# Delta-rule sum tables of a two-block model made by ScalarE copies instead of VectorE products

## The chip, the core and the metric

The kernel runs on one core of a Trainium2 chip. The metric is the device time of one execution in microseconds; the time of a kernel is the median of its runs.

## The reference, cut to what matters

Two transformer blocks follow one another over 512 tokens of width 1024, all in float32. The first block mixes tokens in two ways at once: a gated delta rule (4 heads of 128, chunks of 64 tokens) and a sparse attention (compressed, selected and windowed keys), followed by a feed-forward part. The second block is attention with relative bias, a convolution, and a feed-forward part. The change touches the delta rule, of which this is the part that matters:

```python
gcum = jnp.cumsum(chunks(g), axis=-1)
gdiff = gcum[..., :, None] - gcum[..., None, :]
dec_strict = jnp.where(strict, jnp.exp(jnp.where(strict, gdiff, 0.0)), 0.0)
dec_incl = jnp.where(incl, jnp.exp(jnp.where(incl, gdiff, 0.0)), 0.0)
lower = bc[..., None] * jnp.einsum('nbhid,nbhjd->nbhij', kc, kc) * dec_strict
gam = jnp.exp(gcum)
...
qk = jnp.einsum('nbhid,nbhjd->nbhij', qc, kc) * dec_incl
q_dec = qc * gam[..., None]
```

Here g is one number per token and head (the log of a decay), and gcum its running sum in a chunk. The exponentials of its differences weigh the products of keys and queries.

## The kernel before, in words

Nearly every large product is made on TensorE (PE) from operands split in two: a rounded high part (`whi`, made by ScalarE from the loaded chunk `raw`, L238) and the rest (`wlo`, made by VectorE, L241), so that one product is three matmuls. Weights come in 512 KB chunks from HBM into three buffers of `raw` (`load`, `chunk`, L282).

The delta rule's preparation is a loop over `c`, four chunks of 128 tokens (L886 on). For each it transposes the keys (`kT`, L888), takes the squares of their norms (`rsq`, L878: four small ScalarE squares, a power on GpSimd), and makes the table `rg`: for each of the two parts of g (high and rest, `g2`, L697) and each of the 4 heads, the upper triangle of ones times that head's column of g, 128x128. Four matmuls read the table (`sums_of_g`, L899): two with ones as the other operand give the running sums (`gb`, whose exponential is `gB`, L910), two with a lower triangle give the differences (`gd`, whose exponential is `dm`, L915). PSUM tag `pv` has two buffers, and `rg` has one. Further on in the same step, ScalarE copies the transposed weighted keys (`kbF`, L921; shown in the trace as `h<-tp`), PE makes `qk` and `kk`, and VectorE weighs them with `dm`; the last of these (`a<-sc,dm`, L939 and L940) gives the triangular system that is solved next.

Into this loop, a generator (`side`, L853) mixes independent work in portions: the input products of the sparse attention. Its first part, `nsa_blocks` (L771), makes two products, copies each by ScalarE into four shifted pieces (L782 to L785, `a<-mm` in the trace), adds positions by VectorE (L795, `a<-a,n`), and multiplies the result with the compress weights straight from `raw` (L805, `mm<-raw,a`, 64 matmuls).

The program text gives the priorities, but the order of the instructions on each engine is planned at build time by the framework, which simulates the program (`schedule_with_timeline_sim=True`). On the chip each engine then works through its list in order. Helpers record their own line: nearly all ScalarE work has L238 (`act`), all products and sums of two tensors L241 (`tt`), so tiles tell the steps apart.

Of the kernel before, what the change touches and what calls it, by code (L numbers as in the profile page):

```python
# [6 lines left out]
F32 = mybir.dt.float32  # L7
F32R = mybir.dt.float32r
AF = mybir.ActivationFunctionType
ALU = mybir.AluOpType  # L10
# [191 lines left out]
def body(tc, nc, A, dbg=None, upto=99):  # L202
# [13 lines left out]
    def sb(pool, shape, dt=F32, tag=None, bufs=1):  # L216
        if tag is None:
            nx[0] += 1
            return pool.tile(list(shape), dt, name=f"n{nx[0]}", bufs=bufs)
        return pool.tile(list(shape), dt, name=tag, tag=tag, bufs=bufs)  # L220
# [7 lines left out]
    def ps(tag, shape=(128, 512)):  # L228
        return pp.tile(list(shape), F32, name=tag, tag=tag, bufs=2)
# [7 lines left out]
    def act(out, in_, f, **k):  # L237
        return ACT.activation(out, in_, f, **k)  # L238

    def tt(out, a, b, op, e=None):  # L240
        return (e or DVE).tensor_tensor(out, a, b, op=op)  # L241

    def ts(out, a, s0, s1, op0, op1=None):
        return DVE.tensor_scalar(out, a, s0, s1, op0=op0, op1=op1) if op1 else DVE.tensor_scalar(out, a, s0, None, op0=op0)

    def stt(out, a, s, b, op0, op1):
        return DVE.scalar_tensor_tensor(out, a, s, b, op0=op0, op1=op1)  # L247

    def mm(out, l, r, start=True, stop=True, **k):
        return PE.matmul(out, lhsT=l, rhs=r, start=start, stop=stop, **k)  # L250

    def bc(ap, shape):
        return ap.to_broadcast(shape)
# [354 lines left out]
    B4 = [128, 4, 128]  # L608
# [20 lines left out]
    def r4(ap):  # L629
        return ap.rearrange("p (h c) -> p h c", h=4)  # L630

    def b4(ap):
        return bc(ap[:, :, None], B4)
# [30 lines left out]
    G = {k: ap.bitcast(F32) for k, ap in GR.items()}  # L664
# [31 lines left out]
    g2 = sb(pA, [128, 2, QT, 4], F32R)  # L696
# [163 lines left out]
    def tr4(src, e_out, tag):  # L860
        b = ps(tag, B4)
        for h in range(4):
            PE.transpose(b[:, h], src[:, h], ident)  # L863
        if e_out is not None:
            act(e_out, b, AF.Copy)
        return b

    def tok(c):
        return slice(c * 128, (c + 1) * 128)
# [4 lines left out]
    def pr(ap):  # L874

        return ap.rearrange("p a (h n) -> p a h n", h=2)

    def rsq(i, x):  # L878

        r2 = rqk[:, i, c]  # L880
        for h in range(4):
            act(sb(p1, [128, 128], F32, "jk", 2), x[:, h], AF.Square, accum_out=r2[:, h:h + 1])
        ts(r2, r2, 4 * EPS, None, ALU.add)
        POOL.tensor_tensor(r2, r2, mhalf[:, :4], op=ALU.pow)

    for c in range(QT):  # L886
        kF, qF, vF = (U[nm][:, :, tok(c)] for nm in "kqv")
        kT = tr4(kF, None, "sc")  # L888
        side.run(0.75)
        rsq(0, kT)  # L890
        knc = r4(kn[:, c])
        tt(knc, kT, b4(rqk[:, 0, c]), ALU.mult)
        kb = sb(p1, B4, F32, "h2", 2)
        tt(kb, knc, b4(beta[:, c]), ALU.mult, POOL)
        rg = sb(p1, [128, 2, 4, 128], F32R, "rg", 1)
        for i in range(2):
            tt(rg[:, i], bc(G["triu"][:, None, :], B4), b4(g2[:, i, c].bitcast(F32)), ALU.mult)

        def sums_of_g(o, l):  # L899
            for i in range(2):  # L900
                mm(o.rearrange("p h n -> p (h n)"), l, rg[:, i].rearrange("p h n -> p (h n)"),
                   start=i == 0, stop=i == 1)

        vT = tr4(vF, None, "sc")
        side.run(0.75)
        tt(r4(vb[:, c]), vT, b4(hb[:, c]), ALU.mult)
        gb = ps("pv", B4)
        sums_of_g(gb, GR["ones"])
        gB = sb(p1, B4, F32, "gB", 1)
        act(gB, gb, AF.Exp)  # L910
        side.run(0.75)
        gd = ps("pv", B4)
        sums_of_g(gd, GR["sl"])
        dm = sb(p1, B4, F32, "dm", 2)
        act(dm, gd, AF.Exp)  # L915
        side.run(0.75)
        tt(r4(qdF[:, c]), qF, gB, ALU.mult)
        for h in range(4):
            stt(dm[:, h], dm[:, h], rqk[:, 0, c, h:h + 1], G["triu"], ALU.mult, ALU.mult)
        kbF = sb(p1, B4, F32, "h2", 2)  # L920
        tr4(kb, kbF, "tp")  # L921
        side.run(0.75)
        qk = ps("pv", B4)
        for h in range(4):
            mm(qk[:, h], kF[:, h], qF[:, h])
        side.run(0.75)
        tt(r4(qkT[:, c]), qk, dm, ALU.mult)
        rsq(1, tr4(qF, None, "tp"))
        ts(rqk[:, 1, c], rqk[:, 1, c], 128.0 ** -0.5, None, ALU.mult)
        tt(rq2[:, c], rqk[:, 1, c], rqk[:, 1, c], ALU.mult)  # L930
        kk = ps("sc", B4)
        for h in range(4):
            mm(kk[:, h], kF[:, h], kbF[:, h])
        side.run(0.75)

        k2, d2 = (ap.rearrange("p (a h) n -> p a h n", a=2) for ap in (kk, dm))
        for i in range(2):
            hl = slice(64 * i, 64 * i + 64)
            tt(pr(qF[hl, 0:2]), k2[hl, :, :, hl], d2[hl, :, :, hl], ALU.mult)  # L939
        tt(pr(qF[0:64, 2:4]), k2[0:64, :, :, 64:], d2[0:64, :, :, 64:], ALU.mult)  # L940
# [496 lines left out]
    for t in range(4):  # L1437
# [11 lines left out]
        for qt in reversed(range(QT)):  # L1449
            W = (qt + 1) * 128  # L1450
            for g in range(2):
                h = 2 * t + g
# [126 lines left out]
```

## Time and profile before

| | us |
|---|---|
| median of 3 runs | 1549.27 |
| lowest and highest | 1548.56 and 1551.22 |
| the profiled execution | 1548.64 |
| its span | 1546.7 |
| TensorE busy in it | 1496.1 |
| VectorE busy | 938.5 |
| ScalarE busy | 673.2 |

The span is the time from the first to the last instruction that the profiler recorded. Busy times count instructions with work; a wait at the head of an instruction is idle time. In a timeline, neighbours of one kind are merged into one line, whose length is that of the whole group. The number in brackets is how long the engine stood before it, and after the arrow stands what ended that. The granted clock is 1.00 at TensorE's upper level (2.4 GHz) and 0.50 at the lower (1.2 GHz).

### The profile page before, as it was taken

How to read it: one execution, taken by the hardware profiler on the slowest of the kernel's cores; microseconds unless marked ns; L12 is line 12 of the kernel's file. 1: busy time of each engine (PE TensorE's matmuls, PEld its weight loads, DVE VectorE, ACT ScalarE, POOL GpSimd, SP SyncE). 2: the span in 40 equal slices, each digit the busy share in tenths (PEclk: the TensorE clock that was granted, in tenths of full speed). 3: DMA queues.
4: the chain of work that ended last, by engine and by line, in shares of the span. 5: the costliest groups of instructions: out<-in, count | busy, mean ns of one | idle time of the engine just before them, and what ended most of it. 6: DMA issues, size and time to landing. Idle time of an engine off the chain costs nothing.

```text
span 1546.7 us, 19932 instructions
## 1 busy us (share of the span) xinstructions
PE 1496.1 (97%) x7446; PEld 1255.2 (81%) x7446; DVE 938.5 (61%) x1599; ACT 673.2 (44%) x1250; POOL 145.1 (9%) x249
## 2 busy tenths in 40 slices
PE   7998999999999999999999999999989999999997
PEld 6876888888877878888888878888878888888876
DVE  5778754556647559865664456698844444444556
ACT  6443553345524334444454344345742433333434
POOL 2012001000000122200001010020100000000001
PEclk9999999999999999999999999999999999999999
DMA  6314211211044079933379643164610344434785
GB/s 213 97 53 150 69 56 55 69 42 42 1 164 150 30 259 342 323 111 95 109 270 354 260 150 96 55 231 137 244 42 14 116 140 140 143 121 141 270 283 207
DMA packets 65727, 225.85 MB, mean 146 GB/s; under 512 B 8088, under 2 KB 8088, under 8 KB 64864
## 3 DMA queue, kind: packets, MB, share of 16 engines
q1 hardware_dynamic: 47808, 159.27, 30.9%
q0 software_dynamic: 17248, 64.27, 11.5%
q8 instruction: 58, 0.95, 0.2%
q10 hardware_dynamic: 576, 1.05, 0.2%
q14 instruction: 37, 0.30, 0.1%
HBM read 190.73 MB, written 36.46 MB: 147 GB/s over the span
## 4 chain that ended last, share of the span: by engine, by line
PE 85%; DMA 5%; DVE 4%; ACT 3%; issue 1%; POOL 0%; SPq 0%; POOLq 0%; ACTq 0%; DVEq 0%
PE mm L250 34%; PE sc L250 17%; PE pv L250 16%; PE tp L250 15%; DMA raw<-W 2%; DMA raw<-T 2%; PE tp L1120 1%; DVE wlo L241 1%; ACT whi L238 1%; ACT a L238 1%; DVE a L241 1%; PE tp L619 1%; DMA x<-x 0%; PE tp L863 0%; DMA t<-W 0%
## 5 line engine op out<-in xcount | busy, mean ns | idle before, releaser
L238 ACT ACTIVATE whi<-raw 128x1024 fp32r<-128x1024 f32 (+1 forms) x223 | 232.2, 1043 | 411.4 <-issue 112.8
L241 DVE TENSOR_TENSOR wlo<-raw,whi 128x1024 fp32r<-128x1024 f32 (+2 forms) x209 | 250.5, 1201 | 238.1 <-ACT whi L238 229.6
L250 PE MATMUL mm<-a,whi 128*128 128x512 f32 x608 | 192.8, 396 | 1.1 <-ACT a L238 1.1
L250 PE MATMUL mm<-u,whi 128*128 128x512 f32 x544 | 175.5, 399 | 0.0
L250 PE MATMUL pv<-a,whi 128*128 128x512 f32 (+2 forms) x576 | 160.3, 362 | 1.8 <-ACT a L238 1.2
L250 PEld LDWEIGHTS mm<-a,whi 128*128 128x128 f32 x608 | 115.3, 191 | 25.3 <-ACT a L238 1.3
L250 PE MATMUL mm<-a,wlo 128*128 128x512 f32 x304 | 120.2, 395 | 3.0 <-DVE wlo L241 3.0
L250 PEld LDWEIGHTS pv<-a,whi 128*128 128x128 f32 x576 | 104.2, 189 | 18.9 <-ACT a L238 2.1
L250 PEld LDWEIGHTS mm<-u,whi 128*128 128x128 f32 x544 | 101.2, 190 | 19.4
L250 PE MATMUL tp<-a,whi 128*128 128x512 f32 x368 | 113.9, 390 | 0.0
L250 PE MATMUL mm<-u,wlo 128*128 128x512 f32 x272 | 107.6, 396 | 0.0
L250 PE MATMUL sc<-a,whi 128*128 128x512 f32 x336 | 104.3, 390 | 0.0
L250 PE MATMUL pv<-a,wlo 128*128 128x512 f32 (+2 forms) x288 | 103.7, 361 | 0.0
L247 DVE SCALAR_TENSOR_TENSOR n<-n,n,n 128x511 f32<-128x511 f32 (+23 forms) x120 | 84.6, 734 | 4.2 <-ACT n L238 2.3
L250 PEld LDWEIGHTS tp<-a,whi 128*128 128x128 f32 x368 | 69.1, 188 | 14.3
L250 PE MATMUL sc<-a 128*128 128x128 f32 (+4 forms) x288 | 71.5, 345 | 2.7 <-DVE st L1115 2.7
L250 PEld LDWEIGHTS sc<-a,whi 128*128 128x128 f32 x336 | 63.3, 188 | 13.1
L250 PE MATMUL tp<-a,wlo 128*128 128x512 f32 x184 | 71.6, 389 | 0.0
L250 PEld LDWEIGHTS mm<-a,wlo 128*128 128x128 f32 x304 | 57.9, 190 | 15.4 <-DVE wlo L241 3.4
L250 PEld LDWEIGHTS pv<-a,PT 128*128 128x128 f32 x480 | 63.5, 193 | 8.1 <-ACT PT L238 3.5
L250 PE MATMUL pv<-a,PT 128*128 128x64 f32 x480 | 64.2, 270 | 2.9 <-ACT PT L238 1.7
L250 PE MATMUL sc<-a,wlo 128*128 128x512 f32 x168 | 65.4, 389 | 0.0
(375 smaller groups left out, 2839.3 us busy)
## 6 DMA issues: line engine op xcount, KB each, us to landing
raw<-W SPq DMA_DIRECT2D x227, 512.0 KB, 3.7
a<-W SPq DMA_DIRECT2D x22, 512.0 KB, 6.2
low<-a POOLq DMA_DIRECT2D x22, 512.0 KB, 6.5
raw<-T SPq DMA_DIRECT2D x20, 512.0 KB, 4.8
S<-sp POOLq DMA_DIRECT2D x33, 256.0 KB, 3.2
wlo<-low POOLq DMA_DIRECT2D x14, 512.0 KB, 3.9
a<-S POOLq DMA_DIRECT2D x6, 1024.0 KB, 7.5
w<-W SPq DMA_DIRECT2D x22, 256.0 KB, 5.3
```

What stands on the lines that cost most here:

```text
L238: return ACT.activation(out, in_, f, **k)
L241: return (e or DVE).tensor_tensor(out, a, b, op=op)
L247: return DVE.scalar_tensor_tensor(out, a, s, b, op0=op0, op1=op1)
L250: return PE.matmul(out, lhsT=l, rhs=r, start=start, stop=stop, **k)
L619: PE.transpose(b[:, j, :], src[:, k * 128:(k + 1) * 128], ident)
L1120: PE.transpose(b[:, k * 128:(k + 1) * 128], p_[:, k * 128:(k + 1) * 128], ident)
```

## The change

The table is no longer made by two VectorE products for each chunk (one for each part of g, 128x512, the triangle and the column of g both broadcast), but by eight ScalarE copies, one for each part and head (128x128), each of which reads the triangle and multiplies it by the head's column of g as its scale. Shape, type and the single buffer of `rg` stay, and so does all that reads it.

```diff
@@ -894,7 +894,8 @@
         tt(kb, knc, b4(beta[:, c]), ALU.mult, POOL)
         rg = sb(p1, [128, 2, 4, 128], F32R, "rg", 1)
         for i in range(2):
-            tt(rg[:, i], bc(G["triu"][:, None, :], B4), b4(g2[:, i, c].bitcast(F32)), ALU.mult)
+            for h in range(4):
+                act(rg[:, i, h], G["triu"], AF.Copy, scale=g2[:, i, c, h:h + 1].bitcast(F32))
```

## Rows read from the trace of the kernel before

**Rows 1.** Busy line of the page: busy us, share of the span, instructions of each engine

```profile
PE 1496.1 (97%) x7446; PEld 1255.2 (81%) x7446; DVE 938.5 (61%) x1599; ACT 673.2 (44%) x1250; POOL 145.1 (9%) x249
```

**Rows 2.** Tile view of `rg`: count, ns min/median/max, first and last start, form

```profile
L241 DVE TENSOR_TENSOR rg<-n,n x8: 672/680/694, 100.3 to 126.5; 128x512 fp32r<-128x512 f32 x8
```

**Rows 3.** Windows: us, busy (count) of PE, PEld, DVE, ACT, POOL; clock; DMA, GB/s

```profile
100.00:105.00 5.00, 5.00 (x24) 4.06 (x24) 2.31 (x5) 0.55 (x5) 2.25 (x3) 1.00 0.01 3
105.00:110.00 5.00, 5.00 (x33) 4.30 (x31) 3.35 (x8) 2.17 (x8) 0.88 (x1) 1.00 0.00 0
110.00:115.00 5.00, 4.11 (x30) 3.34 (x29) 4.40 (x13) 4.88 (x13) 1.62 (x3) 1.00 0.00 0
115.00:120.00 5.00, 4.71 (x23) 2.89 (x22) 4.93 (x13) 2.40 (x11) 0.00 (x0) 1.00 0.32 93
...
125.00:130.00 5.00, 3.40 (x27) 2.83 (x26) 4.84 (x14) 3.06 (x16) 1.77 (x3) 1.00 0.32 101
...
140.00:145.00 5.00, 2.33 (x20) 1.93 (x19) 4.77 (x11) 4.37 (x18) 0.62 (x2) 1.00 0.82 232
145.00:150.00 5.00, 5.00 (x19) 3.78 (x18) 4.88 (x16) 0.40 (x4) 3.67 (x3) 0.66 0.63 202
```

**Rows 4.** PE timeline: start us, us, what [idle before <-releaser]

```profile
109.97 0.71 PE L250 MATMUL pv<-rg,n 128*128 128x512 f32 x2
...
111.76 0.71 PE L250 MATMUL pv<-rg,n 128*128 128x512 f32 x2
113.06 0.63 PE L863 MATMUL sc<-n,a 128*128 128x128 f32 x4 [0.58 <-DVE a L241]
...
115.45 1.72 PE L250 MATMUL mm<-raw,a 128*62 128x256 f32 x7 [0.29 <-DVE a L241]
...
126.03 1.16 PE L250 MATMUL pv<-a 128*128 128x128 f32 x8 [0.78 <-DVE a L241]
...
144.75 0.81 PE L863 MATMUL sc<-n,a 128*128 128x128 f32 x4 [2.67 <-DVE a L241]
```

**Rows 5.** DVE timeline, the same columns

```profile
112.84 1.06 DVE L241 TENSOR_TENSOR a<-a,n 128x248 f32<-128x248 f32 x2
...
114.23 0.68 DVE L241 TENSOR_TENSOR rg<-n,n 128x512 fp32r<-128x512 f32 x1
114.83 1.04 DVE L241 TENSOR_TENSOR a<-a,n 128x248 f32<-128x248 f32 x2
115.80 0.67 DVE L241 TENSOR_TENSOR rg<-n,n 128x512 fp32r<-128x512 f32 x1
...
125.90 1.28 DVE L241 TENSOR_TENSOR rg<-n,n 128x512 fp32r<-128x512 f32 x2
...
142.16 1.23 DVE L241 TENSOR_TENSOR wlo<-raw,whi 128x1024 fp32r<-128x1024 f32 x1
143.30 1.30 DVE L241 TENSOR_TENSOR a<-sc,dm 64x256 f32<-64x256 f32 x3
```

**Rows 6.** ACT timeline, the same columns

```profile
107.10 0.60 ACT L238 ACTIVATE gB<-pv 128x512 f32<-128x512 f32 x1 [6.55 <-PE pv L250]
107.60 0.59 ACT L238 ACTIVATE dm<-pv 128x512 f32<-128x512 f32 x1
108.92 0.60 ACT L238 ACTIVATE h<-tp 128x512 f32<-128x512 f32 x1 [0.73 <-PE tp L863]
...
110.44 1.81 ACT L238 ACTIVATE a<-mm 64x512 f32<-64x512 f32 x3
...
113.37 0.58 ACT L238 ACTIVATE gB<-pv 128x512 f32<-128x512 f32 x1
...
121.53 0.60 ACT L238 ACTIVATE gB<-pv 128x512 f32<-128x512 f32 x1 [4.09 <-PE pv L250]
```

**Rows 7.** ACT groups by form, whole kernel: busy us, mean ns of one, idle before

```profile
L238 ACT ACTIVATE a<-a 64x128 f32<-64x128 f32 x56 | 17.3, 310 | 11.5 <-DVE a L241 10.6
...
L238 ACT ACTIVATE P<-P,st 128x128 f32<-128x128 f32 x24 | 9.5, 397 | 4.5 <-DVE st L1115 4.4
```

## The prediction

> **What bounds the kernel now.** I read the page's busy line first: TensorE (PE) is busy 97% of a span of 1546.7 us, VectorE (DVE) 61%, ScalarE (ACT) 44% [rows 1]. So over the whole kernel only PE's idle time can be won, 50.6 us (1546.7 less 1496.1), and a busy stretch of DVE or ACT counts only where PE waits for it. The table `rg` is made four times, once per chunk of 128 tokens, and the tile view says where: eight DVE instructions of about 680 ns, the first at 100.3 us and the last at 126.5 us [rows 2]. Therefore I read the windows from 100 to 150 us next [rows 3]. The reader should see three things there. PE is short of full by 0.89 + 0.29 + 1.60 + 2.67 = 5.45 us. DVE is the fullest engine beside PE (4.40, 4.93 and 4.84 of 5 us in three of the windows). And ACT, which is half idle in most windows, has 4.88 of 5 us in one of them, 110 to 115 us. The last window has a granted clock of 0.66: right after PE stood still for 2.67 us the clock fell to its lower level (1.2 GHz) for most of that window, which costs 5 x 0.34 = 1.7 us of PE work. All that the change can win in this stage by way of PE's waits is then about 5.45 + 1.7 = 7.2 us, or 0.46% of the kernel.
>
> Then the PE timeline, to see who ends those waits [rows 4]: 0.58 us at 113.06, 0.29 at 115.45, 0.78 at 126.03 and 2.67 at 144.75, each ended by a DVE result. I looked at what DVE did just ahead of each [rows 5]. At 115.45 PE begins the long compress matmuls, which need the additions `a<-a,n` at 112.84 and 114.83; a table instruction (114.23) stands between those two. A second one (115.80) follows, and both lie in a DVE run that goes on to the result that PE takes at 126.03. At 144.75 it is `a<-sc,dm` (143.30), which stood in line behind `wlo<-raw,whi` (142.16), a weight split; no table is near.
>
> **What the change does, part by part.**
> Removed: 8 DVE instructions of 0.68 us, 5.4 us of DVE time [rows 2]. In a row two of them take 1.28 us [rows 5]. Chunk 0's and chunk 1's fall in 100 to 110 us, where DVE has 2.31 and 3.35 of 5 us and PE is full [rows 3], so their removal shortens no wait. Chunk 2's two (114.23 and 115.80) take about 1.28 us out of a full DVE. Chunk 3's (125.90) take another 1.28, ahead of work that PE needs only after 128 us.
>
> Added: 32 ACT copies of 128x128, 8 for each chunk, each with a scale read from a column. No row shows exactly this. Below it lies the copy of 128 columns without such an operand, 310 ns; the nearest is the exponential of 128x128 from SBUF with a column as bias, 397 ns [rows 7]. I take 397 ns, since source, size and operand kind agree. Two ACT instructions of one stream can overlap: `dm` begins 0.50 us after `gB`, which lasts 0.60, while the copies `a<-mm` in a row do not (three of them in 1.81 us) [rows 6]. So 8 copies cost 8 x (0.397 - 0.10) = 2.4 us at least and 8 x 0.397 = 3.2 us at most, and I take 3.2, since they too write one tile in a row. In all ACT gets 32 x 0.397 = 12.7 us for the 5.4 us that DVE loses.
> The Trainium skill, "ScalarE: Activation LUTs", section "What ACT_TABLE_LOAD costs", gives 186 ns plus 0.833 ns per column, 93 ns more for a column operand and an overlap of 93 ns; my estimate from it is 386 ns each, or 2.4 us for eight in a row. By it the ACT term would sit at the lower end.
>
> Waits: the tile has one buffer, so chunk c+1's first copy waits until PE has read chunk c's table; what before stood behind that wait on DVE now stands on ACT. Behind it there are `dm`, `kbF`, the squares of the norm, and for chunk 1 the compress input copies `a<-mm`. No DMA is issued from ACT here, and SP's and POOL's queues are not touched.
>
> Now each chunk. Chunk 0: ACT stands idle 6.55 us ahead of `gB` (107.10) [rows 6], so 3.2 us fit; if they did not, PE's first table matmul would be late one for one. Cost 0.
> Chunk 1 is the tight one. PE reads its table at 109.97 [rows 4]. ACT can begin when `dm` is done (108.2). Two copies fit ahead of `kbF` (108.92), and `kbF` with the squares takes until 110.44 [rows 6]; the six other copies (2.4 us) then end at about 112.9. PE has other work until about 111.1 (the second pair at 111.76 less the first pair's 0.71) and then waits; but it has an idle hole before 113.06 as it is [rows 4], and the two pairs move into it. What is really pushed is the run of `a<-mm`: its first four, 0.60 us each, begin at 112.9 instead of 110.44 and end, with `gB` (0.58) among them, at about 115.9. The last two additions (1.06 us, as at 112.84) then end at 116.96, and the compress matmuls begin there instead of at 115.45: 1.5 us lost. Its lower end is 0, if the planner puts `a<-mm` first and the table behind it; the upper end is 3.2 us, all eight copies ahead with no hole to use. I take 1.5.
> Chunk 2: ACT is idle 4.09 us ahead of 121.53 [rows 6]. The copies now fall there, behind an ACT run that ends some 2.5 us later than before, and PE has compress matmuls to do. Cost 0; if that cover were gone, up to 3.2 us.
> Chunk 3: ACT is at 3.06 of 5 us in 125 to 130 [rows 3], 3.2 us more is 6.3, so this table ends after 130 us rather than at 127. PE waits in that window anyway (1.60 us) and has compress work behind it. Cost 0, with an upper end of about 1.3 us, the overflow of the window.
> Gain: with 1.28 us out of the DVE run between 114 and 126 us, the wait of 0.78 us at 126.03 goes; PE is late next by the 0.82 us or so left of that window's 1.60, which the table does not set. The 0.29 at 115.45 is inside the 1.5 above.
>
> The sum: +1.5 - 0.78 = +0.7 us. The profiled run took 1548.64 us, 1.9 more than its span, and it lies 0.63 below the median of 1549.27. So 1548.64 + 0.7 = 1549.3, and with 0.63 a median of about 1550.0.
>
> **The rivals.**
> *Faster: DVE was the bound, and the standstill at 144.75 goes too.* If DVE's 2.6 us for chunks 2 and 3 reach the end of the chain, `a<-sc,dm` (143.30) comes ahead of the weight split (142.16) and PE does not stand: 2.67 + 1.7 + 0.78 = 5.1 us less, 1549.3 - 5.1 = 1544.2. For it: DVE is the fullest engine beside PE in three of the windows, the order on each engine is planned anew, and one place in the queue decides. Against it: that split waits for weights, not for DVE, and no table stands near.
> *Slower: ACT becomes the bound from 108 to 118 us.* ACT has 4.88 of 5 us at 110 to 115, and 3.2 us come in. From the point at which all eight copies stand ahead of the first `a<-mm` and PE's hole grows beyond the 2.67 us that dropped the clock at 144.75, the price is 3.2 + 1.7 = 4.9 us: 1549.3 + 4.9 = 1554.2. For it: the copies depend on nothing but the free buffer, so the planner may issue them early. Against it: they are small pieces, and other work can go between.
> A rule that speaks for this rival is in the Trainium skill, "ScalarE: Activation LUTs", "Rules for kernel authors": a plain multiplication belongs on VectorE, not on ScalarE. The trace agrees as far as sums go (12.7 us for 5.4).
> *Nothing: both engines' changes stay under PE.* The four pairs slide, PE's holes are refilled from the compress matmuls, and the time is 1549.3. This lies within my forecast's band and can't be told from it.
> That the change does not do what it says is not to be expected: both forms name their engine.
>
> **How the numbers follow.** About 0.2% (3.1 us) is what a measurement of this kernel can tell from no change. The forecast with "nothing" beside it: 0.52. Faster: 0.23, of which most is the standstill. Slower: 0.25, the ACT rival, with a new standstill elsewhere in it. The range reaches to 1544.0, the faster rival, and to 1556.0, the slower one plus chunk 3's 1.3 us.
>
> **What would show it.** In the profile after: `rg` in ACT's rows, x32, at about 0.4 us; DVE less by about 5.4 us and ACT more by about 12.7. If step "chunk 1" is right, PE waits for ACT between 110 and 117 us and the compress matmuls begin at 116 to 117. If the wait at 126 still stands, the gain was wrong. If PE does not stand near 145 us, and the clock holds there, the faster rival has won. I am wrong altogether if PE's idle time changes mostly after 150 us, where the table is not used: then the new order, not the engines' load, sets the time.

## The result, and the profile after

The kernel with ScalarE's tables takes 1558.26 us (median; 1557.57 to 1558.82). Beside runs of the kernel before, with a median of 1549.51, that is a ratio of 1.0057, 95% interval 1.0041 to 1.0072: slower by 8.75 us, where 1550.0 us was forecast and 1556.0 was the upper end. The profiled execution took 1558.14 us.

The page's first lines after, span and busy line, answer [rows 1]:

```profile
span 1556.4 us, 19950 instructions
PE 1497.7 (96%) x7446; PEld 1255.4 (81%) x7446; DVE 930.9 (60%) x1591; ACT 683.4 (44%) x1282; POOL 142.0 (9%) x249
```

The span grew by 9.7 us, while PE's busy time grew by 1.6 only, so PE stood longer. VectorE (DVE) lost 7.6 us and ScalarE (ACT) gained 10.2, where 5.4 and 12.7 were forecast: the copies overlap, so that all 32 are 10.2 us of busy time, and of VectorE's loss some 2 us lie outside the table. The tile view of `rg` after answers [rows 2]:

```profile
L238 ACT ACTIVATE rg<-n,n x32: 386/402/419, 100.5 to 130.5; 128x128 fp32r<-128x128 f32 x32
```

To see where the time went, I cut the span into three stretches. The windows' columns are those of [rows 3]. First the kernel before, then the kernel after:

```profile
100.00:140.00 40.00, 37.08 (x202) 26.49 (x202) 30.15 (x73) 17.23 (x60) 10.70 (x13) 1.00 0.30 91
140.00:170.00 30.00, 27.33 (x137) 22.60 (x136) 23.33 (x51) 16.19 (x45) 6.66 (x8) 0.94 0.36 108
170.00:300.00 130.00, 128.82 (x772) 112.92 (x771) 73.82 (x166) 58.50 (x132) 11.03 (x12) 0.99 0.19 59
```

```profile
100.00:140.00 40.00, 35.50 (x188) 25.06 (x187) 25.71 (x64) 24.99 (x90) 10.81 (x13) 1.00 0.23 71
140.00:170.00 30.00, 22.18 (x110) 17.39 (x110) 19.91 (x47) 12.38 (x39) 5.35 (x8) 0.83 0.32 106
170.00:300.00 130.00, 128.47 (x773) 112.27 (x772) 72.41 (x165) 60.99 (x131) 9.49 (x12) 1.00 0.19 60
```

PE's busy time is the one to follow. From 100 to 140 us, where the tables are made, PE is short of full by 2.92 us before and 4.50 after, 1.6 more. From 140 to 170 us, where no table is made or read, it is short by 2.67 before and 7.82 after, 5.15 more; and the granted clock falls from 0.94 to 0.83. What the lower level (1.2 GHz) costs is busy time times what the clock lacks of 1, added up over windows of 1 us: 1.7 us before and 3.0 after. So this stretch lost 5.15 + 1.3 = 6.5 us of the 9.7. From 170 to 300 us, 1.3 us come back (1.18 us of idle time and one fall of the clock, 1.7 us, before; 1.53 us and no fall after). Beyond 300 us PE's idle time grows by 1.2 us and what the clock costs by 0.7, and about 1 us of the 9.7 this account does not place. I draw nothing from that part: in 29 executions of the kernel before, the mean granted clock lies between 0.985 and 0.992 and the span between 1542.7 and 1551.6 us, so as much changes from one execution to the next.

Finer windows of the kernel after, to lay beside [rows 3]:

```profile
110.00:115.00 5.00, 3.65 (x23) 2.50 (x22) 3.17 (x10) 4.95 (x16) 0.61 (x2) 1.00 0.00 0
115.00:120.00 5.00, 3.94 (x21) 2.41 (x20) 4.95 (x13) 4.90 (x15) 0.00 (x0) 1.00 0.10 29
...
125.00:130.00 5.00, 4.62 (x32) 3.67 (x32) 4.23 (x11) 4.52 (x18) 1.33 (x4) 1.00 0.42 134
...
140.00:145.00 5.00, 4.83 (x30) 3.22 (x29) 1.66 (x3) 2.76 (x11) 0.20 (x1) 1.00 0.50 178
145.00:150.00 5.00, 0.76 (x6) 0.42 (x4) 4.66 (x11) 3.21 (x11) 2.45 (x4) 0.92 0.89 306
150.00:155.00 5.00, 1.59 (x8) 1.57 (x8) 4.93 (x14) 0.61 (x2) 1.08 (x1) 0.50 0.37 114
```

The forecast's tight place, 110 to 120 us, is there: ACT is full. But the hole is at 145 to 155 us, where PE works 2.35 of 10 us, DVE is full and ACT is idle for most of it. PE's timeline of both kernels shows what stands there. Before (with [rows 4], where the standstill of 2.67 us at 144.75 is):

```profile
134.90 3.67 PE L250 MATMUL mm<-raw,a 128*62 128x256 f32 x16
138.49 0.66 PE L863 MATMUL tp<-n,h 128*128 128x128 f32 x4
...
145.48 0.47 PE L817 MATMUL mm<-n,a 62*128 62x62 f32 x2
145.89 1.22 PE L250 MATMUL mm<-u,whi 128*128 128x512 f32 x2
```

After:

```profile
116.41 5.39 PE L250 MATMUL mm<-raw,a 128*62 128x256 f32 x24 [1.06 <-DVE a L241]
...
140.40 0.66 PE L863 MATMUL tp<-n,h 128*128 128x128 f32 x4
...
141.43 1.94 PE L250 MATMUL mm<-raw,a 128*62 128x256 f32 x8
...
153.41 1.11 PE L863 MATMUL tp<-n,h 128*128 128x128 f32 x4 [6.59 <-POOL h L241]
...
155.35 0.47 PE L817 MATMUL mm<-n,a 62*128 62x62 f32 x2
155.75 1.22 PE L250 MATMUL mm<-u,whi 128*128 128x512 f32 x2
```

The order is another one, in two places. Before, all compress matmuls (`mm<-raw,a`) are done by 138.6, then come the transposes of chunk 2's weighted keys and of its queries (`tp<-n,h`, `tp<-n,a`). After, those transposes stand at 140.40, and compress matmuls follow them until 143.4: `x8`, which is four matmuls, since the trace has two records for each of these (64 for the 32 in the program). And before, PE goes from chunk 2 to the transposes of the compressed keys (`mm<-n,a`, L817; "compress transposes" below) and to a long run of key products (`mm<-u`) at 145.89; after, chunk 3's key transposes stand ahead of both, and the key products begin at 155.75. PE waits 6.59 us for the operand `h` of chunk 3's key transposes, which GpSimd (POOL) makes. Who made POOL late is read in DVE's timeline after:

```profile
143.03 1.23 DVE L241 TENSOR_TENSOR wlo<-raw,whi 128x1024 fp32r<-128x1024 f32 x1 [4.45 <-ACT whi L238]
...
148.95 1.23 DVE L241 TENSOR_TENSOR wlo<-raw,whi 128x1024 fp32r<-128x1024 f32 x1 [0.30 <-ACT whi L238]
...
151.50 0.69 DVE L241 TENSOR_TENSOR a<-sc,n 128x512 f32<-128x512 f32 x1
...
154.89 0.40 DVE L247 SCALAR_TENSOR_TENSOR a<-a 62x256 f32<-62x256 f32 x1
```

POOL's `h` needs `a<-sc,n` (151.50), which stands in DVE's list behind a weight split that waited 0.30 us for its weights (148.95). The last step of compress' activation (154.89) ends at 155.29, and the compress transposes follow at 155.35. The first key products' weights, high and rest, were done at 144.3 (143.03 + 1.23). So, as far as these weights go, PE stood with work at hand that lay further back in its list (whether PSUM had room for it no row shows).

### The profile page after: what moved, and what is told of

Same layout as the page of the kernel before. It is cut to its first block, busy times and chain, and to the rows that moved or that the text cites. A ratio compares the mean times of both kernels' runs of the same rounds, so it can differ in the third digit from the quotient of the medians.

```text
span 1556.4 us, 19950 instructions
## 1 busy us (share of the span) xinstructions
PE 1497.7 (96%) x7446; PEld 1255.4 (81%) x7446; DVE 930.9 (60%) x1591; ACT 683.4 (44%) x1282; POOL 142.0 (9%) x249
## 4 chain that ended last, share of the span: by engine, by line
PE 86%; DMA 5%; DVE 4%; ACT 3%; issue 1%; POOL 0%; SPq 0%; POOLq 0%; ACTq 0%; DVEq 0%
PE mm L250 34%; PE sc L250 18%; PE pv L250 16%; PE tp L250 15%; DMA raw<-W 2%; DMA raw<-T 2%; PE tp L1121 2%; DVE wlo L241 1%; ACT a L238 1%; PE tp L619 1%; DVE a L241 1%; ACT whi L238 0%; PE tp L863 0%; DMA x<-x 0%; DVE n L241 0%
```

## The experiments

Two theories were put against each other. *Load*: what counts is how much ACT and DVE have to do around 110 to 130 us, and the hole at 145 to 155 is that delay passed on. *Order*: the table's cost on the engines is small, and the loss is that the planner, given other durations, writes another list for PE. Where an edit fixes an order, it uses this helper; it adds no wait for data, it only tells the planner to put the instructions of `later` behind `first` on their engine:

```diff
+    def behind(later, first):
+        for i in later:
+            tc.add_manual_dep(i.ins, first.ins.name, mybir.DependencyInfo(
+                mybir.DependencyClass.NoSync, mybir.DependencyReason.DATA), reason="order")
```

In the edits, `REC["kb", c]`, `REC["q", c]` and `REC["v", c]` are the key (weighted), query and value transposes of chunk c, `HP[1]` the compress matmuls of the second product, `FILL[0]` and `FILL[1]` the matmuls of the first and the second key product, `XH[1]` the last step of compress' activation. Lines of these kernels stand 10 or 17 further down (L827 is L817, L880 is L863).

**e1, after, with the key products ahead of chunk 3's transposes.**

```diff
+    behind(REC["kb", 3] + REC["q", 3], FILL[1][-1])
```

> The changed kernel, with one thing pinned by order-only edges: chunk 3's transposes of the weighted keys and of the queries stand behind the first two key products (mm<-u) on PE, as in the kernel before; the compress transposes (L817) still stand ahead of those products. Theory 'order, narrow' (chunk 3's transposes alone block PE): the 6.6 us standstill goes, about 1551. Theory 'order, wide' (the compress transposes also wait, for a gelu chain that DVE ended at 155.3 in the changed kernel): the standstill only changes its name, 1556 to 1558. Theory 'load' (12.7 us more on ACT is what costs): 1558, and PE's waits are for ACT.

Measured: 1559.35 us, ratio 1.0075 (1.0055 to 1.0094). PE's timeline:

```profile
155.33 0.47 PE L827 MATMUL mm<-n,a 62*128 62x62 f32 x2 [8.59 <-DVE a L247]
```

The wait for POOL is gone, and PE stands 8.59 us for compress' activation in its place, until the same 155.3. So the order theory fell in its narrow form, that this one change of place is the loss; the wide form, that compress was put late too, held, at a time somewhat above its bounds. *Load* gave a time as near (1558), but with waits for ACT, and this one is for DVE.

**e2, after, with DVE's order fixed as well.**

```diff
+    behind(INV[2] + [KN[3], LOS[MARK[1] + 1]], XH[1])
+    behind(REC["kb", 3] + REC["q", 3], FILL[1][-1])
```

The first line puts the start of chunk 2's system (`INV`), chunk 3's key weighing (`KN`) and one weight split (`LOS`) behind compress' activation.

> The changed kernel, all tables on ACT, with the order of the kernel before restored at two places by order-only edges: on PE chunk 3's transposes behind the two key products, on DVE the compress gelu ahead of chunk 2's inverse start, of chunk 3's key scaling and of the third weight split. Theory 'order': 8 us come back, 1549.5 to 1552.5, with PE short by about 4.5 us from 100 to 140 us as in the changed kernel, and nothing like 6 us at 147 to 153. Theory 'load': 1556 to 1559.

Measured: 1558.38 us, ratio 1.0067 (1.0041 to 1.0092). In PE's timeline the standstill is still there, if smaller:

```profile
150.64 0.47 PE L827 MATMUL mm<-n,a 62*128 62x62 f32 x2 [3.94 <-DVE a L247]
```

The expected recovery did not come, and the time lies in the range of *load*. From 140 to 170 us PE loses 7.9 us, idle time and clock together, against 10.9 in the kernel after; but from 170 to 300 us it loses 5.5 against 1.5, so the gain is gone again. Compress' matmuls themselves end at 143.3 in this kernel, as in the kernel after, and neither fix touches that; that this is why so little was won is argued here, and e9 tests it.

**e3, before, with the first key product put behind chunk 3's transposes.**

```diff
+    behind(FILL[0], REC["q", 3][-1])
```

> The kernel before, all tables on DVE, with the changed kernel's order at one place on PE: the first key products behind chunk 3's transposes of the weighted keys and queries. No table is moved. Theory 'order': PE reaches the transposes at 146 and their operand is there at 150.8, so it stands 4 to 5 us and the clock stays low longer: 1553 to 1556. Theory 'load': 1549.5, as before.

Measured: 1550.87 us, ratio 1.0027 (1.0010 to 1.0044), less than expected. PE's timeline shows the wait of the kernel after, made without a single ScalarE table:

```profile
151.68 1.11 PE L880 MATMUL tp<-n,h 128*128 128x128 f32 x4 [4.82 <-POOL h L241]
```

From 140 to 170 us it loses 6.3 us more than the kernel before, idle time and clock together, but from 170 to 300 us 2.7 us less: around 231 to 233 us, where the kernel before stands 1.18 us and its clock falls, key products that are left over fill the hole. A loss in one stretch is not the whole kernel's loss.

**e4 and e6, parts of the change: chunk 2 alone, and chunks 0 to 2, on ScalarE.**

```diff
-            tt(rg[:, i], bc(G["triu"][:, None, :], B4), b4(g2[:, i, c].bitcast(F32)), ALU.mult)
+            if c not in (2,):
+                tt(rg[:, i], bc(G["triu"][:, None, :], B4), b4(g2[:, i, c].bitcast(F32)), ALU.mult)
+                continue
+            for h in range(4):
+                act(rg[:, i, h], G["triu"], AF.Copy, scale=g2[:, i, c, h:h + 1].bitcast(F32))
```

In e6 the list is `(0, 1, 2)`.

> Only chunk 2's table is made by ACT (8 copies), the other three by DVE as before. The planner then gives PE the changed kernel's order at chunk 3 all the same (transposes ahead of compress transposes and key products). Theory 'order': most of the loss with a quarter of the copies, 1554 to 1559. Theory 'load': a quarter of it, 1551 to 1552.

> Chunks 0, 1 and 2 on ACT, chunk 3 by DVE: the same 24 copies as in the run without chunk 1. The planner keeps the key products ahead of chunk 3's transposes on PE, but puts the compress gelu late on DVE, behind chunk 2's mask and the weight splits, while its transposes stand ahead of the key products on PE. Theory 'order': PE stands at the compress transposes, 4 to 8 us, 1553 to 1557. Theory 'load': 1554, with the loss spread over 100 to 140 us. The two are told apart by where PE stands.

Measured: e4 1555.07 us, ratio 1.0046 (1.0029 to 1.0063); e6 1552.66, ratio 1.0027 (1.0009 to 1.0045), just below the bounds of *order*. In both, compress matmuls stand behind chunk 2's transposes. PE's timeline of e4, then of e6:

```profile
138.66 1.94 PE L250 MATMUL mm<-raw,a 128*62 128x256 f32 x8
...
151.52 1.11 PE L863 MATMUL tp<-n,h 128*128 128x128 f32 x4 [5.51 <-POOL h L241]
```

```profile
140.04 1.51 PE L250 MATMUL mm<-raw,a 128*62 128x256 f32 x6
...
151.44 0.47 PE L817 MATMUL mm<-n,a 62*128 62x62 f32 x2 [3.12 <-DVE a L247]
```

A quarter of the change, in a place where ACT had room, brings four fifths of its loss. That speaks against the load. e6 loses 5.4 us more than the kernel before from 140 to 170 us and, like e3, 2.9 us less from 170 to 300.

**e5 and e11, the other parts: chunks 0, 2 and 3, and chunk 1 alone.** The same edit with the lists `(0, 2, 3)` and `(1,)`.

> Chunks 0, 2 and 3 on ACT (24 of the 32 copies, 9.6 us more on ACT), chunk 1 by DVE as before. Here the planner keeps the order of the kernel before at chunk 3 on PE (compress transposes, key products, then chunk 3's transposes) and on DVE (the gelu ahead of chunk 2's mask of kk). Theory 'order': no loss, 1546 to 1550. Theory 'load': three quarters of the loss, about 1554. Theory 'chunk 1' (only ACT's full stretch at 108 to 118 us costs): also 1546 to 1550, with less idle of PE from 100 to 140 us than the 2.9 us of before.

> Only chunk 1's table on ACT; the planner keeps the order of before at chunk 3. It measures the step 'chunk 1' of the prediction by itself: compress matmuls begin 0.5 to 1.5 us later than at 115.45 and PE is short by 1 to 2 us more from 100 to 140 us than the 2.9 of before; time 1548 to 1550.5. Theory 'load' with a quarter of the copies: 1550.

Measured: e5 1546.25 us, ratio 0.9982 (0.9969 to 0.9995); e11 1548.38, ratio 0.9993 (0.9983 to 1.0003). Both have the order of before. In e5 24 of the 32 copies are on ScalarE, three times as many as in e4, and it has the lowest time of the study. That lead itself is not explained by the tables: in its trace PE loses 1.8 us more than before from 100 to 300 us, and what its execution wins lies beyond 300 us, in falls of the clock (6.1 us against 10.5). Its window from 110 to 120 us, and PE's timeline:

```profile
110.00:120.00 10.00, 8.37 (x54) 6.32 (x53) 9.91 (x27) 9.86 (x31) 1.59 (x3) 1.00 0.04 5
```

```profile
136.61 2.37 PE L250 MATMUL mm<-raw,a 128*62 128x256 f32 x10
138.91 0.66 PE L863 MATMUL tp<-n,h 128*128 128x128 f32 x4
```

DVE and ACT are both full there (9.91 and 9.86 of 10 us), and from 100 to 140 us PE is short of full by 2.5 us, no more than before (2.9). e11 gives the price of the tight chunk under the old order; PE's timeline has the start of its compress matmuls:

```profile
116.16 4.96 PE L250 MATMUL mm<-raw,a 128*62 128x256 f32 x22 [0.72 <-DVE a L241]
```

They begin 0.7 us later than before, and from 100 to 140 us PE is short of full by 3.85 us, 0.9 more than before.

**e7, the split into heads without the move: eight VectorE products per chunk.**

```diff
-            tt(rg[:, i], bc(G["triu"][:, None, :], B4), b4(g2[:, i, c].bitcast(F32)), ALU.mult)
+            for h in range(4):
+                ts(rg[:, i, h], G["triu"], g2[:, i, c, h:h + 1].bitcast(F32), None, ALU.mult)
```

> All four tables head by head, eight instructions of 128x128 for each chunk as in the change, but on DVE (triangle times a column), not on ACT. The planner keeps the order of before at chunk 3 on PE and DVE. Theory 'order': 1546 to 1550, since DVE has about as much to do as before. A theory by which many small instructions cost by themselves: 1555 or more.

Measured: 1547.53 us, ratio 0.9996 (0.9976 to 1.0015). The tile view of `rg`:

```profile
L244 DVE TENSOR_SCALAR rg<-n,n x32: 269/274/288, 101.7 to 131.1; 128x128 fp32r<-128x128 f32 x32
```

One takes 0.274 us, but in a row they overlap (eight in 1.66 us): the 32 are 6.8 us of busy time, where the eight products of before are 5.2, on the fullest engine beside PE. Neither the grain of the work nor 1.6 us more on DVE costs anything that the interval can tell; the order was that of before.

**e8 and e12, the first key product ahead of chunk 3's value transposes, in the kernel before and in e5.**

```diff
+    behind(REC["v", 3], FILL[0][-1])
```

> The kernel before with one order-only edge on PE: chunk 3's transposes of the values stand behind the first key product, whose weights are split by 141 us. The standstill of 2.67 us ahead of 144.75 should go, with the low clock behind it: theory 'order' says 2 to 4.4 us less than before, 1544 to 1546.5; if the fill that is used here is missed at its end at 232 us, 0 to 2 us of it come back. Theory 'load': 1548, no change.

> A version meant to beat both: chunks 0, 2 and 3 on ACT, chunk 1 on DVE, and chunk 3's transposes of the values behind the first key product on PE. Theory 'order': the standstill of about 3 us at 142 us gets shorter, 1543 to 1546; if PE only stands at the compress transposes instead, 1545 to 1547.

Measured: e8 1547.62 us, ratio 0.9992 (0.9977 to 1.0007); e12 1548.32, ratio 0.9995 (0.9983 to 1.0006), against e5's 0.9982. Both lie above the time that *order* gave first (1546.5 and 1546 at most), and nothing that the intervals can tell is won. PE's timeline of e8:

```profile
145.45 0.33 PE L827 MATMUL mm<-n,a 62*128 62x62 f32 x2 [3.04 <-DVE a L247]
```

The standstill at 144.75 [rows 4] has two causes in a row: with the value transposes out of the way, PE waits for the compress transposes until almost the same time.

**e9 and e10, the one place that e1 to e6 point to, set in both directions.** e9 is the kernel after with chunk 2's transposes behind the last compress matmul (the order of before); e10 is the kernel before with the last four compress matmuls behind chunk 2's transposes (the order of after).

```diff
+    behind(REC["kb", 2] + REC["q", 2], HP[1][-1])
```

```diff
+    behind(HP[1][-4:], REC["q", 2][-1])
```

> The changed kernel, all 32 copies on ACT, with a single order-only pin on PE: chunk 2's transposes of the weighted keys and queries stand behind the last compress matmul, as they do in the kernel before. With it the planner puts everything behind that place in the order of before (gelu early on DVE, compress transposes, key products, then chunk 3's transposes). Theory 'one place in PE's order': 1548 to 1551 (before plus the 1.6 us that the full ACT costs from 100 to 140 us). Theory 'load': 1555 to 1559.

> The kernel before, all tables on DVE, with the mirror of that pin: the last compress matmuls stand behind chunk 2's transposes, as in the changed kernel. The planner then also puts chunk 3's transposes ahead of the key products. Theory 'one place in PE's order': 1553 to 1557, without a single table moved, with PE standing 5 to 8 us at 143 to 155. Theory 'load': 1548.

Measured: e9 1550.39 us, ratio 1.0003 (0.9993 to 1.0013); e10 1557.46, ratio 1.0048 (1.0036 to 1.0060). The stretches of e9, then those of e10:

```profile
100.00:140.00 40.00, 35.51 (x189) 24.93 (x188) 25.30 (x64) 24.72 (x88) 10.80 (x13) 1.00 0.24 75
140.00:170.00 30.00, 26.22 (x130) 21.09 (x129) 20.20 (x44) 15.62 (x44) 6.59 (x8) 0.94 0.40 129
```

```profile
100.00:140.00 40.00, 37.10 (x198) 26.41 (x197) 30.31 (x72) 16.93 (x61) 10.68 (x13) 1.00 0.28 84
140.00:170.00 30.00, 21.89 (x111) 17.69 (x110) 21.26 (x51) 12.95 (x41) 5.36 (x8) 0.83 0.29 99
```

Read across: from 100 to 140 us e9 is the kernel after (35.51 and 35.50 us of PE) and e10 the kernel before (37.10 and 37.08). From 140 to 170 us it is the other way round: e9 has 26.22 and the clock of before, e10 21.89 and the clock of after. PE's timeline, e9 and then e10:

```profile
139.48 2.37 PE L250 MATMUL mm<-raw,a 128*62 128x256 f32 x10
141.78 0.66 PE L880 MATMUL tp<-n,h 128*128 128x128 f32 x4
...
149.50 1.22 PE L250 MATMUL mm<-u,whi 128*128 128x512 f32 x2
```

```profile
152.31 1.11 PE L880 MATMUL tp<-n,h 128*128 128x128 f32 x4 [5.09 <-POOL h L241]
```

One place in PE's list makes the loss with VectorE's tables and takes it away with ScalarE's:

| tables made by | compress matmuls ahead of chunk 2's transposes | four of them behind |
|---|---|---|
| VectorE | 1 (the kernel before) | 1.0048 (e10) |
| ScalarE | 1.0003 (e9) | 1.0057 (after) |

Down the columns ScalarE's tables cost 0.03% and 0.09%, less than the intervals can tell from nothing; along the rows the place costs 0.48% and 0.54%. The planner plans the rest around the place that is fixed, so it carries followers: in e9 the key products are again ahead of chunk 3's key transposes, in e10 behind them, without having been told. The weights of the key products are a rival: in the kernel after they land later. In e9 they land as late, and the loss is gone. ACT's timeline has the first copy of them, before, after and in e9:

```profile
138.62 1.06 ACT L238 ACTIVATE whi<-raw 128x1024 fp32r<-128x1024 f32 x1 [3.03 <-DMA raw<-W]
...
141.94 1.06 ACT L238 ACTIVATE whi<-raw 128x1024 fp32r<-128x1024 f32 x1 [8.09 <-DMA raw<-W]
...
141.64 1.06 ACT L238 ACTIVATE whi<-raw 128x1024 fp32r<-128x1024 f32 x1 [8.14 <-DMA raw<-W]
```

The followers are not the whole of it either: undoing them alone in the kernel after wins nothing (e1), and making them alone in the kernel before costs 1.0027 (e3).

## Why the prediction was wrong

The step that failed is the assumption under the whole sum, that PE's list stays as it was. Chunks 2 and 3 were costed at nothing because "PE has compress matmuls to do" and "has compress work behind it". That cover is in the trace of before; in the kernel after, the compress matmuls themselves were moved. The prediction wrote down that "the order on each engine is planned anew", but used it in favour of the faster rival alone, and its last part, "the new order, not the engines' load, sets the time", had neither a price nor a chance. That sentence is what came true: 6.5 of 9.7 us were lost between 140 and 170 us, where no table is used. A rival with that mechanism could have been priced from rows: a standstill of 2.67 us and 1.7 us of clock behind it were there [rows 3, 4], and one more of that size, 4.4 us, gives 1553.7 and a larger chance of slower.

Point by point, by PE's shortfall in windows:

- *Chunk 1, +1.5 us.* Right in kind and near in size, but by another path. Between 110 and 120 us the shortfall grew from 0.89 + 0.29 to 1.35 + 1.06, by 1.2 us. The compress matmuls begin at 116.41 (116.96 was forecast, 115.45 before). The step had DVE's additions wait for ACT's `a<-mm`; but DVE has no wait for ACT from 110 to 120 us: when the turn of the additions came (114.50 and 115.81), their `a<-mm` were there. What came late was `kbF` (`h<-tp`): seven copies went ahead of it, not two, and it begins at 111.45 instead of 108.92. The products that read it (`sc`) came late on PE, and DVE stood for them ahead of `a<-sc,dm` and the additions. That the size comes near is luck. DVE's timeline after:

```profile
113.27 1.31 DVE L241 TENSOR_TENSOR a<-sc,dm 64x256 f32<-64x256 f32 x3 [1.68 <-PE sc L250]
```

- *Chunk 2's gain, -0.78 us at 126.03.* Right for that wait: it is gone. The shortfall from 125 to 130 us fell further, from 1.60 to 0.38, because the other 0.82 us moved past 130 us (0.61 at 130.91, below); 0.34 us of waiting for POOL's `h`, at 125.76, is new.
- *Chunk 3, 0 with an upper end of 1.3.* Mis-sized: from 130 to 140 us PE was full before and stood 1.71 us after. Of that, 0.61 is the wait that moved here, 0.72 stands at the table's own matmuls, until ACT's `gB` was done, and 0.37 at compress transposes, until DVE's activation was. In e5, with chunk 3 on ScalarE but chunk 1 not, PE is full in that window, so it takes chunk 1's delay together with the overflow. PE's timeline after:

```profile
130.91 0.63 PE L863 MATMUL sc<-n,a 128*128 128x128 f32 x4 [0.61 <-DVE a L241]
...
132.50 0.72 PE L250 MATMUL pv<-rg,n 128*128 128x512 f32 x2 [0.72 <-ACT gB L238]
```

- *The sum for 100 to 140 us*, +0.7, measured +1.6. e9, with all tables on ScalarE and the old place, measures 1.0003 (-1.1 to +2.0 us); +0.7 and +1.6 both lie in that interval. So the part about load is small, as forecast, had the list stood; which of the two sizes it has, the times don't tell.
- *The price of a copy.* 397 ns were taken from [rows 7], 402 were measured. Where I chose 3.2 us for eight in a row, the other end was right. ACT's timeline after:

```profile
111.45 0.58 ACT L238 ACTIVATE h<-tp 128x512 f32<-128x512 f32 x1
111.92 0.39 ACT L238 ACTIVATE rg<-n,n 128x128 fp32r<-128x128 f32 x1
...
112.72 4.85 ACT L238 ACTIVATE a<-mm 64x512 f32<-64x512 f32 x8
...
119.06 2.45 ACT L238 ACTIVATE rg<-n,n 128x128 fp32r<-128x128 f32 x8
```

  Eight take 2.45 us, one every 0.29 us, so they do overlap. The Trainium skill, "ScalarE: Activation LUTs", section "What ACT_TABLE_LOAD costs", gives 93 ns of overlap and led to an estimate of 386 ns and 2.4 us; the trace agrees (402 ns, 2.45 us).
- *The rivals.* The faster one, "the standstill at 144.75 goes", fell: e8 shows that a second wait stands behind the first. The slower one foresaw a new standstill with a fall of the clock, but put it at ACT around 110 to 118 us; it came at 145 to 155, with ACT idle for 6 us of 10. Its point of decision, all copies ahead of the first `a<-mm`, was reached (the eighth copy ends at 112.3, 111.92 + 0.39, and the first `a<-mm` begins at 112.72), and cost 1.2 us there, not 4.9. Both rivals' times also count a term twice: 1549.3 already holds the 0.78 that the faster one takes off again (1545.0 without that), and chunk 1's 1.5, which the slower one's 3.2 takes the place of (1552.7).
- *A rule that spoke for the slower rival*, multiplication belongs on VectorE ("Rules for kernel authors", same page of the Trainium skill), does not decide here: e5, with 24 such products on ScalarE, measures 0.9982 (0.9969 to 0.9995), no slower than the kernel before, though one such product takes 402 ns on ScalarE and 274 on VectorE (e7).

What stays open: why the planner moved those four matmuls. It happens with chunk 2 alone (e4) and, with three of them, with chunks 0 to 2 (e6), and not with chunks 0, 2 and 3 (e5) or chunk 1 alone (e11), so it does not follow the amount of work. It is decided when the program is built, and no run shows it. Of the 9.7 us of span, some 3 lie beyond 300 us or are not placed at all, and were not traced to these matmuls.

## What to carry to other kernels

In a kernel whose lists are planned at build time, a change of an engine is two changes: the work and the new lists. Cost the second one as well, as a standstill of the size that the trace already has, and look first at the order on the busiest engine once the new kernel is there; an edge that fixes one place, set in both directions, tells order from load with two runs. When the tables on their own are harmless, choosing which of them move (e5) can avoid the loss that moving all brings.

## What the runs showed of the hardware

- ScalarE's copies of 128x128 with a scale from a column overlap when they stand in a row, one every 0.29 us at 402 ns each, though they write one tile. In the same kernel the eight copies `a<-mm` (64x512, from PSUM) take 4.85 us, one every 0.61 us at 592 ns each, and do not.
- VectorE multiplies 128x128 by a column in 274 ns, eight in a row in 1.66 us (e7), against 680 ns for one product of 128x512 with broadcast operands [rows 2] and 1.28 us for two [rows 5]: splitting costs DVE 30% (6.8 us of busy time against 5.2) and the kernel nothing that the runs can tell (0.9976 to 1.0015).
- After the standstills of 145 to 153 us the granted clock was 0.50 from 150 to 155 us, TensorE's lower level, with PE at work for 1.59 us only in that window. The standstill, not the level, was the larger loss: 5.15 us against 1.3.
